# Branch A begun with two column tiles of half the tokens, and the entry of the FFN with its evictions, splits and sums in another order

## The chip, the core and the metric

The kernel runs on one core of a Trainium2 chip. The core has five engines that run side by side and meet through semaphores: TensorE (PE in the profile) multiplies matrices, VectorE (DVE) and ScalarE (ACT) work element by element, GpSimd (POOL) does a few element-wise operations and roots here, and SyncE (SP) only issues DMAs; ACT issues some too. PE writes its results to PSUM, which has eight banks of 128 partitions by 512 floats; everything else lies in SBUF. The metric is device time in microseconds (us) of one execution; lower is better.

## The reference, cut to what matters

One layer of a transformer-like block over 1024 tokens with 1024 channels, in float32. The two places that are changed lie behind the attention.

```python
y_a = stick_breaking_attention(q, k, v)
y_b = cb * causal_dwconv(cc * cx, conv_w[l])
merged = (jax.nn.sigmoid(ga) * (y_a @ w_branch_a[l])          # branch A
          + jax.nn.sigmoid(gb) * (y_b @ w_branch_b[l]))       # branch B
x = x + g1 * (merged @ w_out[l])                              # out-projection
h = rmsnorm(x, ln2_g[l]) * (1.0 + sc2) + sh2                  # FFN entry
f = (jax.nn.silu(h @ w_ffn_gate[l]) * (h @ w_ffn_up[l])) @ w_ffn_down[l]
return x + g2 * f
```

## The kernel before

**Products.** A float32 product is made of three matmuls: each operand is split into a high and a low part (`hi` is a rounded copy made by ACT, `lo` is the operand less `hi`, made by DVE), and `hi*hi`, `hi*lo` and `lo*hi` are summed in one PSUM bank. A matmul can therefore wait for an ACT copy or for the DVE subtraction behind it. In tile names `whi` and `wlo` are the parts of a weight; `rh`, `rl` and `big` hold those of activations.

**Branch A** (L1025 to L1042) computes, for each of eight column tiles `m` of the weight `w_a` and each half `n` of the tokens, one bank of 24 matmuls (eight blocks `k` of the inner dimension by three; `mm_ch`, L876 to L878). Two banks (`pj`) are there for it. DVE empties a bank with a multiplication by the gate (L1036: tile `sgi`, loaded by SP from DRAM, two buffers), adds branch B's part (L1037: tile `mb`, also a load) and ACT and DVE split the sum into `big` (L1041, L1042). A gate's buffer is free for the load after next once L1042 has read it. The operands `ya` come from the attention, whose last blocks for `n` = 1 are read back by SP (`yr`, L1017) and split (L1021 and its subtraction) while branch A is already running. A scheduler sets the order of instructions on each engine from the order of the source, with estimated costs and the buffers that are free; it already mixes the banks of (m, n) = (0, 1) and (1, 0).

**FFN entry** (from L1179). The out-projection goes over eight token tiles `i`. Each gives a new residual tile `x1`, an RMS norm (ACT squares and sums, L1209; POOL makes the root; ACT rescales, L1213), eight transposes on PE (`tail_tr`, L1094) into two banks, one for each half `g` of the channels, and eight evictions of 128x128 that scale and shift (`tail_ev`, ACT L1104 and DVE L1106) into the buffers `h2b`. `h2b` is a table of four: channel half by token half, names h2b00, h2b01, h2b10, h2b11. `tail_f` then does DVE subtractions between these and splits one (`rh[2]`, `rl[2]`, L1115).

The FFN's weights and activations are cut two by two, and each block product is formed with seven half-size products instead of eight, as in Strassen's scheme (Winograd's form). That takes sums of blocks: T3 = h2b11 - h2b00 (split into `rh[6]`, `rl[6]`, used by product 7) and T4 = h2b10 - h2b11 (split into `rh[3]`, `rl[3]`, used by product 4). A product is 12 matmuls (`half_prod`, L127 to L129). The first gate step's products are written by hand in the entry: `pq[1]`, `pq[2]`, then `pre[0, 1]`, `pre[1, 0]`, `pre[1, 1]` of three further weight tiles (their raw tiles `w_u[0]`, `w_g[1]`, `w_u[1]`, whose split halves are `s01`, `s10`, `s11`), then `pq[6]`, `pq[5]`, `pq[3]`, `pq[7]`; product 4 opens `strassen(0, 0)` behind it. `x1p`, `x11`, `x2p`, `x21` (tile name `wt`) collect partial results.

What stands between `i0` (at the last tile of the out-projection) and `in_order(i0)` (L1268) keeps, on each engine, the order in which it is written; the scheduler orders the rest around it. In the loop over gate steps behind it, ACT applies Silu to each gate tile (L1336), and POOL forms the sums of weight blocks (`ws`, L132) for gate steps from the second on.

Of the kernel before, what the change touches and what calls it, by code (L numbers as in the profile page):

```python
# [28 lines left out]
def block_kernel(tc, x, x_t, cols, ada_1, ada_2, ada_row, w_q, w_kv, w_v1, w_cg, w_a, w_b, w_o, w_g, w_u, w_d, out):  # L29
# [992 lines left out]
            tt(nc.vector, l_, yr, h_.bitcast(F32), ALU.subtract)  # L1022
            yah[n][k], yal[n][k] = h_, l_
    mh, mlo = [None] * 2, [None] * 2
    for m in range(KT):  # L1025
        if m == KT - 2:
            preload_wo()
        w = load_ch(w_a[m])
        for n in range(2):
            sa = fp.tile([P, 512], F32, tag="sgi", bufs=2, name=nm("sgi"))  # L1030
            nc.sync.dma_start(sa, d_sga[m, :, n * 512:(n + 1) * 512])
            mb = fp.tile([P, 512], F32, tag="st", bufs=3, name=nm("mb"))
            nc.sync.dma_start(mb, d_mb[m, :, n * 512:(n + 1) * 512])
            ps = ps_f()
            mm_ch(ps, w, yah[n], yal[n])
            nc.vector.tensor_tensor(out=sa, in0=ps, in1=sa, op=ALU.mult)  # L1036
            nc.vector.tensor_tensor(out=sa, in0=sa, in1=mb, op=ALU.add)  # L1037
            if m == 0:
                mh[n] = big()
                mlo[n] = big()  # L1040
            nc.scalar.activation(mh[n][:, m, :], sa, AF.Copy)  # L1041
            nc.vector.tensor_tensor(out=mlo[n][:, m, :], in0=sa, in1=mh[n][:, m, :].bitcast(F32), op=ALU.subtract)  # L1042
# [37 lines left out]
    def split_big(dh, dl, src, t=None):  # L1080

        if t is None:
            cuts = [(slice(k, k + 2), slice(0, 512)) for k in (0, 2)]
        else:
            cuts = [(slice(0, 4), slice(t * P, t * P + P))]
        for c in cuts:
            nc.scalar.activation(dh[:, *c], src[:, *c], AF.Copy)  # L1087
            tt(nc.vector, dl[:, *c], src[:, *c], dh[:, *c].bitcast(F32), ALU.subtract)
# [5 lines left out]
                nc.tensor.transpose(trs[g][:, j * P:(j + 1) * P], xn[:, (4 * g + j) * P:(4 * g + j + 1) * P], ident)  # L1094
        return trs

    def tail_ev(i, trs, acts=(0, 2)):
        n, t0 = i // 4, (i % 4) * P
        for g in range(2):
            for j in range(4):  # L1100
                k = 4 * g + j
                o, s = h2b[g][n][:, j, t0:t0 + P], trs[g][:, j * P:(j + 1) * P]
                if j in acts:
                    nc.scalar.activation(o, s, AF.Identity, scale=a2[:, k:k + 1], bias=mod[:, 2, k:k + 1])  # L1104
                else:
                    nc.vector.tensor_scalar(out=o, in0=s, scalar1=a2[:, k:k + 1], scalar2=mod[:, 2, k:k + 1],  # L1106
                                            op0=ALU.mult, op1=ALU.add)
# [44 lines left out]
    for ch in range(2):  # L1152
# [21 lines left out]
        for i in (0, 4, 1, 2, 3, 5, 6, 7) if ch else range(8):  # L1174
# [29 lines left out]
            nc.scalar.dma_start(x1[:, :512], d_x1[i, :, :512])  # L1204
            nc.vector.tensor_tensor(out=x1[:, cs], in0=tm, in1=xi, op=ALU.add)
# [3 lines left out]
            nc.scalar.activation(xn, x1, AF.Square, accum_out=ss)  # L1209
            r = rstd_of(ss, 1.0 / D, dp, 1)  # L1210
            if last:
                s01 = halves(load_raw(w_u[0]))
            nc.scalar.activation(xn, x1, AF.Copy, scale=r[:, 0:1])  # L1213
            tails.append((i, xn))
            if last:
# [17 lines left out]
    x1p, x11 = wt(1), wt(0)  # L1233
    nc.scalar.activation(x1p, pq[1], AF.Copy)
    tt(nc.vector, x11, pq[2], x1p, ALU.add)
    s10 = halves(load_raw(w_g[1]))
    trs7 = tail_tr(tails.pop()[1])
    s6.close()

# [15 lines left out]
    nc.scalar.activation(x2p, pre[0, 1][0], AF.Copy)
# [14 lines left out]
    s7 = ExitStack()  # L1270
    cp = s7.enter_context(tc.tile_pool(name="phc2", bufs=1, side="right", reuse_waits="tile"))
# [305 lines left out]
```

## Time and profile before

| what | value |
|---|---|
| median of 3 runs | 1859.14 us (1858.46 to 1859.62) |
| the profiled execution | 1862.36 us, of which the span of the instructions is 1860.6 us |
| PE busy | 1815.7 us, 98% of the span |
| DVE busy | 1351.7 us, 73% |
| ACT busy | 794.0 us, 43% |
| POOL busy | 369.3 us, 20% |

Times in the views count from the start of the span. A row of a timeline has the start, the duration, the engine, the line of the kernel, the operation, the tile written and the tiles read, the shape and how many alike were joined; in brackets stands how long the engine had been idle before, and what ended it. A duration of one matmul (0.39 us) overlaps the next: back-to-back matmuls of 128x512 start 0.2275 us apart. Likewise an operation of 128x512 on DVE or ACT is shown with 0.6 to 0.7 us and the next starts 0.52 (ACT) or 0.60 us (DVE) after it. Branch A runs from about 1017 to 1117 us, the out-projection to about 1210, the FFN entry to about 1262, the other gate and up products to about 1640, the down-projection to the end.

### The profile page before, as it was taken

The numbers are of one execution on the slowest core, as the hardware profiler recorded it, in microseconds if no ns is written. First come the engines' busy times: TensorE is split into PE (matmuls) and PEld (weight loads), VectorE is DVE, ScalarE is ACT, GpSimd is POOL, SyncE is SP. The second block draws the span as 40 slices with busy tenths as digits, with TensorE's granted clock in tenths as the row PEclk, the third lists the DMA queues.
The fourth block names the chain that finished last, engine by engine and source line by source line (L and its number), as shares of the span: only waits on it lengthen the run. The fifth ranks groups of instructions, "written<-read, shape, count | busy, mean of one in ns | idle before, by whom it ended". The sixth has DMA issues, their size and how long they took to land. (4 is left out here: it accounts for less than half of the span.)

```text
span 1860.6 us, 24885 instructions
## 1 busy us (share of the span) xinstructions
PE 1815.7 (98%) x8829; PEld 1505.1 (81%) x8829; DVE 1351.7 (73%) x1946; ACT 794.0 (43%) x1494; POOL 369.3 (20%) x277
## 2 busy tenths in 40 slices
PE   7999999999999999999999899989999999999999
PEld 4787778887879988888888788868888888878887
DVE  6873776779864888888887545589987787744776
ACT  4352553333343656665565211654444344422321
POOL 1043327423230000000000000104543444300000
PEclk9999999999999999999999999999999999999999
DMA  9598452227748565689544536414443334289766
GB/s 389 197 309 302 161 190 71 85 74 247 275 156 250 151 191 176 178 245 281 147 133 137 187 126 214 138 61 170 177 163 147 136 148 184 110 324 330 284 229 223
DMA packets 147267, 358.01 MB, mean 192 GB/s; under 512 B 15480, under 2 KB 44480, under 8 KB 144968
## 3 DMA queue, kind: packets, MB, share of 16 engines
q1 hardware_dynamic: 101816, 289.12, 46.1%
q10 hardware_dynamic: 44320, 63.64, 9.8%
q0 software_dynamic: 1008, 3.67, 0.5%
q8 instruction: 70, 1.15, 0.3%
q14 instruction: 53, 0.43, 0.1%
HBM read 245.74 MB, written 110.66 MB: 192 GB/s over the span
## 5 line engine op out<-in xcount | busy, mean ns | idle before, releaser
L788 DVE TENSOR_TENSOR_SCAN pt<-pt,mk 128x128 f32<-128x128 f32 (+7 forms) x128 | 172.0, 1350 | 48.2 <-ACT pt L784 48.0
L784 ACT ACTIVATE pt<-z,rq 128x512 f32<-128x512 f32 (+3 forms) x192 | 107.1, 579 | 88.6 <-PE z L783 57.5
L127 PE MATMUL e<-big,whi 128*128 128x512 f32 x352 | 137.7, 391 | 2.6 <-ACT whi L1070 2.5
L129 PE MATMUL e<-big,wlo 128*128 128x512 f32 x352 | 137.4, 390 | 0.9 <-DVE wlo L1071 0.8
L128 PE MATMUL e<-big,whi 128*128 128x512 f32 x352 | 137.2, 390 | 0.0
L118 POOL TENSOR_SCALAR rs_m<-ss 128x1 f32<-128x1 f32 x8 | 2.2, 280 | 661.1 <-ACT xn L1209 661.1
L132 DVE TENSOR_TENSOR c<-e,c 128x512 f32<-128x512 f32 x138 | 92.8, 686 | 53.6 <-PE e L129 51.7
L127 PE MATMUL pj<-big,whi 128*128 128x512 f32 x320 | 125.1, 391 | 1.0 <-DVE c L132 1.0
L128 PE MATMUL pj<-big,whi 128*128 128x512 f32 x320 | 124.7, 390 | 0.0
L129 PE MATMUL pj<-big,wlo 128*128 128x512 f32 x320 | 124.3, 390 | 0.0
L1404 PE MATMUL e<-whi,f 128*128 128x512 f32 (+1 forms) x319 | 121.8, 382 | 1.1 <-DMA f<-d_f 1.1
L1405 PE MATMUL e<-wlo,f 128*128 128x512 f32 (+1 forms) x319 | 121.8, 382 | 0.0
L1406 PE MATMUL e<-whi,f 128*128 128x512 f32 (+1 forms) x319 | 121.6, 382 | 0.0
L132 DVE TENSOR_TENSOR wlo<-raw,whi 128x512 fp32r<-128x512 f32 x116 | 89.1, 772 | 38.0 <-ACT whi L473 37.9
L132 DVE TENSOR_TENSOR c<-pj,c 128x512 f32<-128x512 f32 x140 | 93.2, 682 | 30.8 <-PE pj L129 30.6
L473 ACT ACTIVATE whi<-raw 128x512 fp32r<-128x512 f32 x116 | 72.7, 630 | 97.8 <-PE pj L128 42.8
L290 PE MATMUL pj<-whi,big 128*128 128x512 f32 x352 | 109.7, 398 | 4.2 <-ACT big L273 4.1
L132 POOL TENSOR_TENSOR ws<-raw,raw 128x512 f32<-128x512 f32 x40 | 55.3, 1384 | 287.7 <-DMA raw<-w_cg 126.4
L807 DVE TENSOR_TENSOR atl<-tr,ath 128x512 fp32r<-128x512 f32 (+1 forms) x192 | 99.6, 548 | 14.4 <-ACT ath L806 12.6
L127 PE MATMUL e<-rh,whi 128*128 128x512 f32 x264 | 104.1, 394 | 2.4 <-ACT rh L1087 2.4
L128 PE MATMUL e<-rl,whi 128*128 128x512 f32 x264 | 104.6, 396 | 1.3 <-DVE rl L132 1.3
L806 ACT ACTIVATE ath<-tr 128x512 fp32r<-128x512 f32 (+1 forms) x192 | 86.8, 489 | 44.0 <-PE o L818 25.8
(255 smaller groups left out, 5030.8 us busy)
## 6 DMA issues: line engine op xcount, KB each, us to landing
f<-d_f SPq DMA_DIRECT2D x77, 512.0 KB, 4.3
d_f<-fs SPq DMA_DIRECT2D x70, 512.0 KB, 3.3
raw<-w_cg SPq DMA_DIRECT2D x40, 512.0 KB, 5.1
raw<-w_u SPq DMA_DIRECT2D x26, 512.0 KB, 3.3
raw<-w_g SPq DMA_DIRECT2D x25, 512.0 KB, 3.5
ad<-ada ACTq DMA_DIRECT2D x19, 512.0 KB, 5.6
ada<-ada SPq DMA_DIRECT2D x8, 1024.0 KB, 10.3
d_t<-ts SPq DMA_DIRECT2D x16, 512.0 KB, 5.1
```

Of the source, the lines that this page charges most:

```text
L127: nc.tensor.matmul(ps, wh[:, k, :], fh[:, k, :], start=(k == 0), stop=False)
L128: nc.tensor.matmul(ps, wh[:, k, :], fl[:, k, :], start=False, stop=False)
L129: nc.tensor.matmul(ps, wl[:, k, :], fh[:, k, :], start=False, stop=(k == 3))
L132: eng.tensor_tensor(out=out, in0=a, in1=b, op=op)
L290: nc.tensor.matmul(ps, a, b, start=(k == 0 and q == 0), stop=(k == KT - 1 and q == 2))
L784: nc.scalar.activation(pt[:, off + s0:off + s0 + m], z[:, :m], AF.Sigmoid, scale=rq[:, 1, i, h:h + 1])
L788: nc.vector.tensor_tensor_scan(out=pt[:, rev], data0=pt[:, rev], data1=mk[:, rev], initial=1.0, op0=ALU.mult, op1=ALU.max)
L806: nc.scalar.activation(th[:, :nb, c0:c0 + P], src, AF.Copy)
L807: nc.vector.tensor_tensor(out=tl[:, :nb, c0:c0 + P], in0=src, in1=th[:, :nb, c0:c0 + P].bitcast(F32), op=ALU.subtract)
L1404: nc.tensor.matmul(o, sh, w[0][:, c], start=(j == 0), stop=False)
L1405: nc.tensor.matmul(o, sh, w[1][:, c], start=False, stop=False)
L1406: nc.tensor.matmul(o, sl, w[0][:, c], start=False, stop=(j == NJ - 1))
```

## The change

Three things in the source:

- Branch A takes its first four (m, n) in the order (0, 0), (1, 0), (0, 1), (1, 1) instead of (0, 0), (0, 1), (1, 0), (1, 1).
- `tail_ev` gives all four evictions of channel half `g` = 0 (one bank) to ACT and all four of `g` = 1 (the other bank) to DVE; before, both engines took two from each bank, in turns.
- In the FFN entry, the splits of `w_u[0]` come ahead of the last tile's Square, those of `w_g[1]` ahead of its rescaling, those of `w_u[1]` and of two weight sums (`sp3`, `sp4`) ahead of the last tile's evictions. T3 and T4 are subtracted in two halves of 128x1024 each, both ahead of the splits that read them, and the sum `x1p` comes ahead of T3's low part. The first Silu has to follow the end of the ordered region on ACT and DVE.

```diff
-    for m in range(KT):
-        if m == KT - 2:
+    wa = {}
+    for m, n in [(0, 0), (1, 0), (0, 1), (1, 1)] + [(m, n) for m in range(2, KT) for n in range(2)]:
+        if (m, n) == (KT - 2, 0):
             preload_wo()
-        w = load_ch(w_a[m])
-        for n in range(2):
-            sa = fp.tile([P, 512], F32, tag="sgi", bufs=2, name=nm("sgi"))
...
+        if n == 0:
+            wa[m] = load_ch(w_a[m])
+        sa = fp.tile([P, 512], F32, tag="sgi", bufs=2, name=nm("sgi"))
...
+        mm_ch(ps, wa[m], yah[n], yal[n])
...
-    def tail_ev(i, trs, acts=(0, 2)):
+    def tail_ev(i, trs):
+
         n, t0 = i // 4, (i % 4) * P
-        for g in range(2):
-            for j in range(4):
+        for j in range(4):
+            for g in range(2):
                 k = 4 * g + j
                 o, s = h2b[g][n][:, j, t0:t0 + P], trs[g][:, j * P:(j + 1) * P]
-                if j in acts:
+                if g == 0:
                     nc.scalar.activation(o, s, AF.Identity, scale=a2[:, k:k + 1], bias=mod[:, 2, k:k + 1])
...
+            if last:
+                s01 = halves(load_raw(w_u[0]))
...
             nc.scalar.activation(xn, x1, AF.Square, accum_out=ss)
             r = rstd_of(ss, 1.0 / D, dp, 1)
             if last:
-                s01 = halves(load_raw(w_u[0]))
+                s10 = halves(load_raw(w_g[1]))
             nc.scalar.activation(xn, x1, AF.Copy, scale=r[:, 0:1])
...
-    s10 = halves(load_raw(w_g[1]))
+    s11 = halves(load_raw(w_u[1]))
+    sp3, sp4 = split(ws0[3]), split(ws0[2])
     trs7 = tail_tr(tails.pop()[1])
...
     tail_ev(7, trs7)
     tail_f(7)
     pre[1, 0] = two(*s10)
-    s11 = halves(load_raw(w_u[1]))
     split_big(rh[5], rl[5], h2b[1][1])
-    sp3, sp4 = split(ws0[3]), split(ws0[2])
     pre[1, 1] = two(*s11)
...
-    tt(nc.vector, h2b[0][0], h2b[1][1], h2b[0][0], ALU.subtract)
+    for k in (slice(0, 2), slice(2, 4)):
+        tt(nc.vector, h2b[0][0][:, k], h2b[1][1][:, k], h2b[0][0][:, k], ALU.subtract)
+    tt(nc.vector, x1p, pq[6], x1p, ALU.add)
     split_big(rh[6], rl[6], h2b[0][0])
     pq[7] = product(sp4, 6)
     sp5 = split(load_raw(w_g[NJ])[:, 512:])
-    tt(nc.vector, x1p, pq[6], x1p, ALU.add)
-    tt(nc.vector, h2b[1][0], h2b[1][0], h2b[1][1], ALU.subtract)
+    for k in (slice(0, 2), slice(2, 4)):
+        tt(nc.vector, h2b[1][0][:, k], h2b[1][0][:, k], h2b[1][1][:, k], ALU.subtract)
     split_big(rh[3], rl[3], h2b[1][0])
-    in_order(i0)
+    ends = in_order(i0)
...
-            nc.scalar.activation(o, o, AF.Silu)
+            with tc.issue_after(ends[0]), tc.issue_after(ends[1]):
+                nc.scalar.activation(o, o, AF.Silu)
```

Where this moves instructions, the program's own rows show it. First DVE in branch A, around the evictions of the second and third bank. The bank and gate of (1, 0) are pj 10298 and sgi 10294 before, and 10263 and 10259 after; those of (0, 1) are 10253 and 10249 before, 10296 and 10292 after. Before:

```order
L132 TENSOR_TENSOR ya_2079_10201<-yr_2078_10199,ya_2079_10201 128x512
L1036 TENSOR_TENSOR sgi_2100_10294<-pj_2102_10298,sgi_2100_10294 128x512
L1036 TENSOR_TENSOR sgi_2090_10249<-pj_2092_10253,sgi_2090_10249 128x512
L1037 TENSOR_TENSOR sgi_2100_10294<-sgi_2100_10294,mb_2101_10296 128x512
L132 TENSOR_TENSOR wlo_2110_10367<-raw_2106_10360,whi_2109_10366 128x512
L1037 TENSOR_TENSOR sgi_2090_10249<-sgi_2090_10249,mb_2091_10251 128x512
```

and after (lines here are one higher):

```order
L132 TENSOR_TENSOR ya_2079_10201<-yr_2078_10199,ya_2079_10201 128x512
L1037 TENSOR_TENSOR sgi_2095_10259<-pj_2097_10263,sgi_2095_10259 128x512
L1038 TENSOR_TENSOR sgi_2095_10259<-sgi_2095_10259,mb_2096_10261 128x512
L1037 TENSOR_TENSOR sgi_2098_10292<-pj_2100_10296,sgi_2098_10292 128x512
L1043 TENSOR_TENSOR big_2089_10246<-sgi_2095_10259,big_2088_10245 128x512
L132 TENSOR_TENSOR wlo_2110_10367<-raw_2106_10360,whi_2109_10366 128x512
```

DVE empties (1, 0) first in both; (0, 1) is second in both. SP's rows keep their places, but the load that was for (0, 1)'s gate is now for (1, 0)'s, and the later one the other way round. Before, SP reads:

```order
L1031 DMA sgi_2090_10249<-d_sga_76 128x512
L1033 DMA mb_2091_10251<-d_mb_79 128x512
L1017 DMA yr_2078_10199<-d_ya1_75 128x512
L1033 DMA mb_2101_10296<-d_mb_79 128x512
L1033 DMA mb_2104_10329<-d_mb_79 128x512
L462 DMA raw_2117_10436<-w_a 128x1024
L1031 DMA sgi_2100_10294<-d_sga_76 128x512
```

and after:

```order
L1032 DMA sgi_2095_10259<-d_sga_76 128x512
L1034 DMA mb_2096_10261<-d_mb_79 128x512
L1017 DMA yr_2078_10199<-d_ya1_75 128x512
L1034 DMA mb_2099_10294<-d_mb_79 128x512
L1034 DMA mb_2104_10329<-d_mb_79 128x512
L462 DMA raw_2117_10436<-w_a 128x1024
L1032 DMA sgi_2098_10292<-d_sga_76 128x512
```

The gate that DVE asks for first is the one that SP loads first only after the change.

Second, ACT in the FFN entry, from tile 5's evictions (tiles h2b01 and h2b11) over the last tile's Square (writes xn and ss) to its rescaling (reads rs_r). Before:

```order
L1104 ACTIVATE h2b01_11198<-e_2323_11626,mod_113,a2_10860 128x128
L1104 ACTIVATE h2b11_11199<-e_2324_11627,mod_113,a2_10860 128x128 x2
L1115 ACTIVATE rh2_11193<-h2b11_11199 128x4x128
L1204 DMA x1_2330_11698<-d_x1_82 128x512
L1206 DMA d_x1_82<-x1_2330_11698 128x512
L1209 ACTIVATE xn_2332_11703,ss_2331_11702<-x1_2330_11698 128x1024
L1070 ACTIVATE whi_2336_11711<-raw_2335_11709 128x512
L1070 ACTIVATE whi_2338_11715<-raw_2335_11709 128x512
L1213 ACTIVATE xn_2332_11703<-x1_2330_11698,rs_r_2334_11706 128x1024
```

and after:

```order
L1106 ACTIVATE h2b01_11198<-e_2323_11626,mod_113,a2_10860 128x128 x4
L1217 ACTIVATE xn_2313_11582<-x1_2311_11577,rs_r_2315_11585 128x1024
L1117 ACTIVATE rh2_11193<-h2b11_11199 128x4x128
L1206 DMA x1_2330_11698<-d_x1_82 128x512
L1208 DMA d_x1_82<-x1_2330_11698 128x512
L1071 ACTIVATE whi_2332_11704<-raw_2331_11702 128x512
L1071 ACTIVATE whi_2334_11708<-raw_2331_11702 128x512
L1213 ACTIVATE xn_2337_11713,ss_2336_11712<-x1_2330_11698 128x1024
L1071 ACTIVATE whi_2341_11721<-raw_2340_11719 128x512
L1071 ACTIVATE whi_2343_11725<-raw_2340_11719 128x512
L1217 ACTIVATE xn_2337_11713<-x1_2330_11698,rs_r_2339_11716 128x1024
```

The high parts of `s01` (whi of `w_u[0]`) moved from behind the Square to ahead of it, and those of `s10` took their place.

Third, DVE at the end of the entry, from `rl[5]` (written to a big tile) on. Before, up to T4 (behind it come three low parts of weight sums and `rl[3]`):

```order
L132 TENSOR_TENSOR big_2356_11795<-h2b11_11199,big_2355_11794 128x1024 x2
L1071 TENSOR_TENSOR wlo_2365_11853<-wt_2196_10881,whi_2364_11852 128x512
L1071 TENSOR_TENSOR wlo_2367_11857<-wt_2195_10880,whi_2366_11856 128x512
L132 TENSOR_TENSOR wt_2371_11887<-e_2341_11745,wt_2370_11886 128x512
L132 TENSOR_TENSOR wt_2347_11767<-wt_2371_11887,wt_2347_11767 128x512
L132 TENSOR_TENSOR big_2356_11795<-h2b01_11198,big_2355_11794 128x1024 x2
L132 TENSOR_TENSOR h2b00_11200<-h2b11_11199,h2b00_11200 128x2048
L132 TENSOR_TENSOR rl6_11797<-h2b00_11200,rh6_11796 128x1024 x2
L1071 TENSOR_TENSOR wlo_2378_11954<-raw_2376_11951,whi_2377_11953 128x512
L132 TENSOR_TENSOR wt_2346_11766<-e_2372_11894,wt_2346_11766 128x512
L132 TENSOR_TENSOR h2b10_11201<-h2b10_11201,h2b11_11199 128x2048
```

and after, up to `rl[3]`:

```order
L132 TENSOR_TENSOR big_2365_11813<-h2b11_11199,big_2364_11812 128x1024 x2
L132 TENSOR_TENSOR wt_2371_11887<-e_2346_11755,wt_2370_11886 128x512
L132 TENSOR_TENSOR big_2365_11813<-h2b01_11198,big_2364_11812 128x1024 x2
L132 TENSOR_TENSOR h2b00_11200<-h2b11_11199,h2b00_11200 128x1024 x2
L132 TENSOR_TENSOR wt_2351_11776<-e_2372_11894,wt_2351_11776 128x512
L132 TENSOR_TENSOR rl6_11815<-h2b00_11200,rh6_11814 128x1024 x2
L1072 TENSOR_TENSOR wlo_2378_11956<-raw_2376_11953,whi_2377_11955 128x512
L132 TENSOR_TENSOR h2b10_11201<-h2b10_11201,h2b11_11199 128x1024 x2
L1072 TENSOR_TENSOR wlo_2391_12082<-ws_2198_10883,whi_2390_12081 128x512
L1072 TENSOR_TENSOR wlo_2394_12104<-ws_2197_10882,whi_2393_12103 128x512
L1072 TENSOR_TENSOR wlo_2397_12122<-ws_2199_10884,whi_2396_12121 128x512
L132 TENSOR_TENSOR rl3_11817<-h2b10_11201,rh3_11816 128x1024 x2
```

Two low parts (wlo) and one product of `wt` tiles have left this stretch: the low parts now come ahead of the last tile's evictions, the product behind `rl[3]`. The three low parts of weight sums ahead of `rl[3]` stand there in both.

More of the change, by code (lines that the diff above doesn't have):

```diff
@@ L1024, in block_kernel @@
     mh, mlo = [None] * 2, [None] * 2
-    for m in range(KT):
-        if m == KT - 2:
+    wa = {}
+    for m, n in [(0, 0), (1, 0), (0, 1), (1, 1)] + [(m, n) for m in range(2, KT) for n in range(2)]:
+        if (m, n) == (KT - 2, 0):
             preload_wo()
-        w = load_ch(w_a[m])
-        for n in range(2):
-            sa = fp.tile([P, 512], F32, tag="sgi", bufs=2, name=nm("sgi"))
[L1031 to L1042, printed above, removed]
+        if n == 0:
+            wa[m] = load_ch(w_a[m])
+        sa = fp.tile([P, 512], F32, tag="sgi", bufs=2, name=nm("sgi"))
+        nc.sync.dma_start(sa, d_sga[m, :, n * 512:(n + 1) * 512])
+        mb = fp.tile([P, 512], F32, tag="st", bufs=3, name=nm("mb"))
+        nc.sync.dma_start(mb, d_mb[m, :, n * 512:(n + 1) * 512])
+        ps = ps_f()
+        mm_ch(ps, wa[m], yah[n], yal[n])
+        nc.vector.tensor_tensor(out=sa, in0=ps, in1=sa, op=ALU.mult)
+        nc.vector.tensor_tensor(out=sa, in0=sa, in1=mb, op=ALU.add)
+        if m == 0:
+            mh[n] = big()
+            mlo[n] = big()
+        nc.scalar.activation(mh[n][:, m, :], sa, AF.Copy)
+        nc.vector.tensor_tensor(out=mlo[n][:, m, :], in0=sa, in1=mh[n][:, m, :].bitcast(F32), op=ALU.subtract)
     s3.close()
@@ L1082, in split_big @@
         if t is None:
-            cuts = [(slice(k, k + 2), slice(0, 512)) for k in (0, 2)]
+            cuts = [(slice(k, k + 2), slice(0, 512)) for k in range(0, src.shape[1], 2)]
         else:
```

## The prediction

> **What bounds the kernel now.** I read the page first: PE is busy for 98% of the span, so a gain can only come from its idle time or from its clock.
>
> ```profile
> span 1860.6 us, 24885 instructions
> PE 1815.7 (98%) x8829; PEld 1505.1 (81%) x8829; DVE 1351.7 (73%) x1946; ACT 794.0 (43%) x1494; POOL 369.3 (20%) x277
> ```
>
> Then busy time and granted clock in stretches of 3.41 us at both changed places (columns: stretch, its length, busy time of PE, its weight loads, DVE, ACT, POOL; PEclk; DMA share; GB/s).
>
> ```profile
> 1037.67:1041.09 3.42, 1.23 (x3) 0.48 (x3) 0.69 (x1) 0.87 (x2) 0.00 (x0) 1.00 0.71 240
> 1041.09:1044.50 3.41, 1.22 (x3) 1.03 (x4) 1.96 (x4) 0.04 (x1) 0.00 (x0) 0.50 0.02 9
> 1044.50:1047.91 3.41, 3.41 (x10) 2.67 (x9) 2.42 (x4) 1.22 (x2) 0.00 (x0) 0.50 0.69 219
> ...
> 1249.30:1252.71 3.41, 0.72 (x2) 0.19 (x1) 3.41 (x5) 1.95 (x3) 0.00 (x0) 1.00 0.35 135
> 1252.71:1256.12 3.41, 2.39 (x6) 1.91 (x7) 3.41 (x5) 0.60 (x3) 0.00 (x0) 0.50 0.00 0
> ...
> 1221.99:1225.40 3.41, 2.08 (x14) 1.60 (x12) 3.14 (x6) 2.36 (x5) 0.00 (x0) 1.00 0.00 0
> ```
>
> A long wait is paid twice: after the stretch with PE busy for 1.23 us (36%) the clock is half, and again after the one with 0.72 us (21%); after the one with 2.08 us (61%) it stays full. Half clock lasts until a full stretch has passed.
>
> **Branch A, the wait.** PE's timeline:
>
> ```profile
> 1037.97 0.50 PE L876 MATMUL pj<-ya,whi 128*128 128x512 f32 x1 [1.07 <-ACT ya L1021]
> ...
> 1043.29 0.80 PE L876 MATMUL pj<-ya,whi 128*128 128x512 f32 x1 [3.86 <-DVE sgi L1036]
> ...
> 1048.05 0.40 PE L878 MATMUL pj<-ya,wlo 128*128 128x512 f32 x1
> ```
>
> The eviction that ends the 3.86 us waits itself for a gate (DVE's and SP's timelines, and the loads' times in the view of the tile `sgi`):
>
> ```profile
> 1037.94 0.69 DVE L132 TENSOR_TENSOR ya<-yr,ya 128x512 fp32r<-128x512 f32 x1 [1.83 <-ACT ya L1021]
> 1042.54 1.29 DVE L1036 TENSOR_TENSOR sgi<-pj,sgi 128x512 f32<-128x512 f32 x2 [3.90 <-DMA sgi<-d_sga]
> ```
>
> ```profile
> 1030.66 0.50 SPq L1031 DMA_DIRECT2D sgi<-d_sga  x1
> ...
> 1035.18 0.43 SPq L1031 DMA_DIRECT2D sgi<-d_sga  x1
> ```
>
> ```profile
> DMA to landing us min/median/max: 2.9/3.8/7.2
> ```
>
> The gate issued at 1035.18 is (1, 0)'s. It lands near 1042.5, the longest of its kind, and DVE wants it first. (0, 1)'s gate, issued at 1030.66, has lay there since about 1035 (median 3.8, at most 1037.9), but its eviction stands behind. So both banks stay full.
>
> **What the new order does.** SP's rows stay; the gate of 1030.66 becomes (1, 0)'s, which DVE evicts first. (1, 0) also runs ahead on PE, and its bank is full before (0, 1)'s last block, which still needs the `ya` of 1037.94. DVE therefore evicts (1, 0) right behind that row, at 1037.94 + 0.60 = 1038.54 to 1039.23. PE ends (0, 1) at about 1039.3 as now and goes on with (1, 1) at 1039.3 instead of 1043.29: **4.0 us**. Next is the late gate, now (0, 1)'s: landing still at 1042.5, eviction done at 1043.25. PE wants that bank for (2, 0) after 24 x 0.2275 = 5.46 us, at 1044.75, which leaves 1.5 us. The low part of (1, 0) now stands on DVE behind that late eviction, so the buffer for (1, 1)'s gate is free at 1043.9; issued at 1044 it lands at 1047.8 (median) or 1051.2 (longest), and (2, 1) wants the bank at 1050.2. By the median there is nothing to pay, by the longest 1.7 us. I take nothing.
>
> The second price: 11 starts from 1043.29 to 1048.05 take 4.76 us instead of 11 x 0.2275 = 2.50, so half clock costs 2.26. With no wait above 1.07 us the stretch is busy enough: **2.2 us** back. A start of (0, 1) on a bank that comes free 0.2 us later is deducted: branch A gives 6.0 us; between 2.3 (half clock stays and the late landing is paid: 4.0 - 1.7) and 6.5.
>
> **FFN entry, the waits.** PE's timeline again, then ACT's:
>
> ```profile
> 1217.18 0.50 PE L127 MATMUL e<-big,whi 128*128 128x512 f32 x1 [0.92 <-ACT whi L1070]
> ...
> 1225.64 0.50 PE L127 MATMUL e<-big,whi 128*128 128x512 f32 x1 [1.57 <-ACT whi L1070]
> ...
> 1233.25 0.50 PE L129 MATMUL e<-big,wlo 128*128 128x512 f32 x1 [0.80 <-DVE wlo L1071]
> ...
> 1249.13 0.39 PE L129 MATMUL e<-rh,wlo 128*128 128x512 f32 x1
> 1251.87 0.51 PE L127 MATMUL e<-rh,whi 128*128 128x512 f32 x1 [2.35 <-ACT rh L1087]
> 1253.73 0.80 PE L128 MATMUL e<-rl,whi 128*128 128x512 f32 x1 [1.35 <-DVE rl L132]
> 1254.32 0.63 PE L129 MATMUL e<-rh,wlo 128*128 128x512 f32 x1
> ...
> 1259.44 0.44 PE L129 MATMUL e<-big,wlo 128*128 128x512 f32 x1
> ```
>
> ```profile
> 1209.43 0.79 ACT L1104 ACTIVATE h2b<-e,mod,a 128x128 f32<-128x128 f32 x2
> 1210.70 0.46 ACT L1104 ACTIVATE h2b<-e,mod,a 128x128 f32<-128x128 f32 x1 [0.48 <-DVE h2b L1106]
> ...
> 1215.46 1.06 ACT L1209 ACTIVATE xn<-x 128x1024 f32<-128x1024 f32 x1 [3.19 <-DVE x L1205]
> ...
> 1216.52 1.14 ACT L1070 ACTIVATE whi<-raw 128x512 fp32r<-128x512 f32 x2
> ```
>
> Start to start less 0.2275, with the slower starts behind a stall, the three stalls up to 1233.25 and their small followers cost about 4.6 us. The first is `s01`, behind the Square; the second `s10`, behind the whole of tile 6; the third `s11`, behind tile 7.
>
> The evictions first. In turns on one bank, ACT waits for DVE (0.48) and DVE for ACT, about 0.53 each time. On two banks at once they are 4 x 0.32 = 1.3 us per tile; that both engines read two banks at full speed is not in these rows, so the other bound is the alternation as now. I take 1.3. The Trainium skill ("PSUM — Partial Sum Buffer", specifications) says that ScalarE and VectorE read PSUM in parallel at full bandwidth as long as they don't meet in a bank; by it the first bound would hold and the second fall away. No row here shows that pairing.
>
> With it tile 7's residual is ready about 1.9 us before the 1215.46 at which the Square could start. `s01`'s two highs (1.04) go first, at 1213.6 to 1214.6, and its lows end by 1215.3; PE wants them at 1216.1. The Square starts 1.9 - 1.04 = 0.9 us earlier than now; `s10` covers POOL's root, and `s10` and `s11` are split 5 us or more before their products. All three stalls go, and PE would be at product 4 at 1249.13 + 0.23 - 4.6 = 1244.8.
>
> **FFN entry, the chain on DVE.** DVE's timeline:
>
> ```profile
> 1226.98 0.41 DVE L1106 TENSOR_SCALAR h2b<-e,a,mod 128x128 f32<-128x128 f32 x1
> 1228.78 0.76 DVE L1106 TENSOR_SCALAR h2b<-e,a,mod 128x128 f32<-128x128 f32 x2 [1.39 <-ACT h2b L1104]
> 1230.07 0.41 DVE L1106 TENSOR_SCALAR h2b<-e,a,mod 128x128 f32<-128x128 f32 x1 [0.53 <-ACT h2b L1104]
> ...
> 1233.72 2.36 DVE L132 TENSOR_TENSOR big<-h2b,big 128x1024 fp32r<-128x1024 f32 x2
> 1236.00 1.29 DVE L1071 TENSOR_TENSOR wlo<-wt,whi 128x512 fp32r<-128x512 f32 x2
> 1237.95 0.69 DVE L132 TENSOR_TENSOR wt<-e,wt 128x512 f32<-128x512 f32 x1 [0.67 <-ACT wt L1255]
> ...
> 1244.97 2.36 DVE L132 TENSOR_TENSOR rl<-h2b,rh 128x1024 fp32r<-128x1024 f32 x2 [1.13 <-ACT rh L1087]
> ...
> 1248.45 2.28 DVE L132 TENSOR_TENSOR h2b<-h2b,h2b 128x2048 f32<-128x2048 f32 x1
> ...
> 1252.45 2.36 DVE L132 TENSOR_TENSOR rl<-h2b,rh 128x1024 fp32r<-128x1024 f32 x2
> ```
>
> From tile 7's first eviction to `rl[3]` DVE needs 1252.45 - 1226.98 = 25.5 us. Out of it go the waits for ACT, 1.39 + 0.53 + 0.67 + 1.13 = 3.7 (the last since T3's first half reaches ACT 1.1 us sooner, with `x1p` as cover), the two low parts of `sp3` and `sp4`, 1.2, and the product of `wt` tiles, 0.6: 20.0 remain. The halves cost nothing: two of 128x1024 are 2 x 1.14 (row 1244.97 is such a pair), one of 128x2048 is 2.28. `s11`'s lows leave it too, but then DVE waits as long for ACT's first half of `rh[5]`, which they covered. Tile 7 itself starts earlier by 1.9 (tile 6) + 1.1 (its two alternations) less 1.2 (the low parts now ahead): 1.8, at 1225.2. `rl[3]` starts at 1245.2, and PE's second matmul of product 4, 1.28 us behind as in 1252.45 to 1253.73, at about 1246.2 (the slack of 0.1 us between dependent operations goes with the removed ones). That is 7.6 us before 1253.73; PE, there at 1245.0, still waits some 1.2 us. Bounds: 4.3, where evictions still alternate for three tiles (3 x 1.1 later), and 8.7, where PE finds `rl[3]` ready.
>
> That wait leaves PE busy for at least 2.1 of 3.41 us, like the stretch after which the clock stayed full. Half clock then goes: 12 starts from 1254.32 to 1259.44 take 5.12 us instead of 2.73, **2.4 us**. FFN entry: 7.6 + 2.4 = **10.0 us**.
>
> POOL's sums for the second gate step come next:
>
> ```profile
> 1260.04 1.29 POOL L132 TENSOR_TENSOR ws<-raw,raw 128x512 f32<-128x512 f32 x1 [42.52 <-DMA raw<-w_g]
> ```
>
> Their weight needs a buffer that DVE frees behind `rl[3]`, 7.3 us earlier than now, while PE comes 10.0 earlier: 2.7 us of cover are lost. There are 5.6 now: four sums of 1.3 and a split of 1.2 end at 1266.4, and PE comes to them after product 4 (to 1258.4) and five products of 12 x 0.2275, at 1272.0. The Silu held back with its table load (ACT, about 1.9 us in the middle of the entry) lands where ACT idles. Both at nothing.
>
> **Sum.** 6.0 + 10.0 = 16.0 us. The profiled execution took 1862.36, 1.8 around the span included; it would be 1846.4. The median of the runs is 3.2 lower, 1859.14, and the forecast **1843.1 us**.
>
> **Rivals.**
> - *The clock drops at the wait that is left* (chance 0.15). A wait of 1.2 to 2 us leaves PE busy between 41% and 65% of a stretch, and between 36% and 61% no row tells. Price 2.4, once: 1845.5; in both places 1847.7. The Trainium skill ("TensorE: Matmul & The Clock Gate", Part 1) wants about one idle window of 3.4 us before half clock. By it neither 1037.67 nor 1249.30, in which PE still worked, should have been followed by half clock; they were, so the rows decide.
> - *The late gate is the new wait in branch A* (0.08): it comes 1.5 us later still or (1, 1)'s takes 7.2. PE waits 1.7 and more, half clock with it: branch A gives 2 instead of 6, 1847.
> - *DVE stays the bound of the entry* (0.10): evictions alternate or ACT is late with `rh[3]`; 4.3 instead of 7.6, and half clock stays: 1843.1 + 3.3 + 2.4 = 1848.8.
> - *The change doesn't do what it says* (0.03): the scheduler had already mixed (0, 1) and (1, 0), and T3 and T4 cost DVE as much as before. Then both waits stay: 1859. Against it: the gate that DVE asks for first does change.
> - *Slower, through the clock* (0.04): many short waits in the first gate steps, as POOL's sums come late, hold PE at half clock. Half clock costs 3.41 / 2 = 1.7 us a stretch; from ten stretches in a row (34 us) it eats the 16.0, from twelve it loses 4: 1863. Against it: before, it lasted two stretches each time. The Trainium skill ("TensorE: Matmul & The Clock Gate", A second HAM failure mode) tells of a clock that swings when PE idles briefly between groups; no row here shows it.
>
> **Chances.** The forecast has 0.60, the rivals 0.15, 0.08, 0.10, 0.03 and 0.04. About 0.2% (3.7 us) is what a measurement of this kernel can tell from no change. The first four cases are faster: 0.93; 0.03 the same, 0.04 slower. The range reaches down to 1839.5 (product 4 without a wait, 1.1; branch A's 6.5; and 2 for the difference between a profiled execution and the runs) and up to 1850.5, which holds all faster cases with the same 2 us above the worst.
>
> **What would show it.** After: PE without the wait of 3.86 at L1037's release, (1, 1) starting 4 us sooner, clock 1.00 there; no stall at `s01`, `s10`, `s11`; one wait of about 1.2 us on `rl[3]`. Wrong it would be if a wait on a gate or on POOL's `ws` stood in their place, or half clock at either.

## The result, and the profile after

| kernel | median (runs) | ratio to before, 95% interval |
|---|---|---|
| before | 1859.4 us (4); 1860.9 us (15, in the last comparison) | |
| changed, first comparison | 1848.4 us (4: 1846.7 to 1852.2) | 0.9938 [0.9924, 0.9952] |
| changed, timed again | 1850.3 us (6: 1847.7 to 1852.5) | 0.9945 [0.9932, 0.9957] |

The change makes the kernel some 10.7 us faster; 16.0 were forecast, and 1843.1 us. The time lies within the range, in its upper half; the second timing's median, 1850.3 us, is just below the range's end of 1850.5. The profiled execution took 1846.74 us, the fastest of the changed kernel's ten. The page of after:

```profile
span 1845.0 us, 24888 instructions
PE 1810.0 (98%) x8829; PEld 1504.7 (82%) x8829; DVE 1346.3 (73%) x1948; ACT 792.1 (43%) x1494; POOL 369.1 (20%) x277
```

PE issues the same 8829 matmuls in both kernels, so both timelines of PE can be laid side by side by the number of the matmul. What the changed kernel gains on before's profiled execution between two numbers is what it gains in that place:

| place (numbers of the matmuls) | gain | forecast |
|---|---|---|
| 0 to 5200, programs alike up to branch A | 4.8 us | 0 |
| branch A (5200 to 5400) | 6.3 | 6.0 |
| out-projection (5400 to 6000) | 0.0 | 0 |
| FFN entry up to product 4 (6000 to 6200) | 10.4 | 10.0 |
| next gate steps (6200 to 6400) | -3.8 | 0 |
| start of the down-projection (7800 to 8000) | -2.1 | 0 |

Both places gave what was forecast of them. What was missing stands behind the entry, and in how typical one execution is. PE's timeline of after, all waits at branch A and from the entry on to the third gate step:

```profile
1025.07 0.50 PE L876 MATMUL pj<-ya,whi 128*128 128x512 f32 x1 [0.36 <-DVE mb L948]
1032.96 0.49 PE L876 MATMUL pj<-ya,whi 128*128 128x512 f32 x1 [0.57 <-ACT ya L1021]
1033.69 0.50 PE L877 MATMUL pj<-ya,whi 128*128 128x512 f32 x1 [0.23 <-DVE ya L132]
...
1234.93 0.50 PE L128 MATMUL e<-rl,whi 128*128 128x512 f32 x1 [1.37 <-DVE rl L132]
...
1266.77 0.50 PE L127 MATMUL e<-big,whi 128*128 128x512 f32 x1 [1.63 <-DVE c L132]
...
1271.77 0.50 PE L127 MATMUL e<-big,whi 128*128 128x512 f32 x1 [1.99 <-ACT c L1310]
```

The wait of 3.86 us in branch A is gone, and so are the stalls on the three split weights; on `rl[3]` 1.37 us are left (forecast 1.2). The last two rows are new: each is the first matmul into a PSUM bank that an eviction has just freed. Before, PE came to the second of these banks as it was being freed, and waited some 0.3 us (before's timelines of ACT and of PE):

```profile
1288.85 0.58 ACT L1305 ACTIVATE c<-e 128x512 f32<-128x512 f32 x1
```

```profile
1289.49 0.50 PE L127 MATMUL e<-big,whi 128*128 128x512 f32 x1
```

DVE's timeline of after, first in branch A:

```profile
1032.94 0.69 DVE L132 TENSOR_TENSOR ya<-yr,ya 128x512 fp32r<-128x512 f32 x1 [0.88 <-ACT ya L1021]
1033.55 0.68 DVE L1037 TENSOR_TENSOR sgi<-pj,sgi 128x512 f32<-128x512 f32 x1
...
1037.48 0.69 DVE L1037 TENSOR_TENSOR sgi<-pj,sgi 128x512 f32<-128x512 f32 x1 [2.52 <-DMA sgi<-d_sga]
```

(1, 0) is evicted right behind the last `ya`, as worked out; the late gate, now (0, 1)'s, keeps DVE for 2.52 us, and PE waits for nothing there. Then the queue of DVE and of ACT ahead of the two new waits:

```profile
1260.95 3.48 DVE L132 TENSOR_TENSOR fs<-wt,fs 128x512 fp32r<-128x512 f32 x2
1264.35 1.76 DVE L1072 TENSOR_TENSOR wlo<-ws,whi 128x512 fp32r<-128x512 f32 x1
1266.04 0.68 DVE L132 TENSOR_TENSOR c<-e,c 128x512 f32<-128x512 f32 x1
...
1270.41 0.68 DVE L132 TENSOR_TENSOR fs<-c,fs 128x512 fp32r<-128x512 f32 x1
```

```profile
1271.12 0.60 ACT L1310 ACTIVATE c<-e 128x512 f32<-128x512 f32 x1 [0.17 <-DVE fs L132]
```

The eviction at 1266.04 (`c<-e`) stands behind 5 us of splits of hidden activations (`fs`) and of a weight, which nobody waits for so soon. ACT's copy at 1271.12 wants to write the tile `c1` (tag c10, one buffer), which DVE's split at 1270.41 still reads. The banks are those of `pre[1, 0]` and `pre[1, 1]`, products that the entry makes ahead for the second gate step: they hold four of the eight banks until the first gate step's hidden activations are through (which banks and tiles these are follows from the source and from what ended the waits; the experiment with a second c1 tests it).

### The profile page after: what moved, and what is told of

Its sections match the earlier page's. It is cut to its first block, busy times and chain, and to the rows that moved or that the text cites. A ratio compares the mean times of both kernels' runs of the same rounds, so it can differ in the third digit from the quotient of the medians.

```text
span 1845.0 us, 24888 instructions
## 1 busy us (share of the span) xinstructions
PE 1810.0 (98%) x8829; PEld 1504.7 (82%) x8829; DVE 1346.3 (73%) x1948; ACT 792.1 (43%) x1494; POOL 369.1 (20%) x277
## 4 chain that ended last, share of the span: by engine, by line
PE 80%; DVE 11%; DMA 5%; issue 2%; ACT 2%; POOL 1%; SPq 0%; ACTq 0%; DVEq 0%; POOLq 0%
PE e L129 7%; PE e L128 7%; PE e L127 7%; PE pj L290 5%; PE pj L127 5%; PE pj L129 5%; PE pj L128 5%; PE pj L876 4%; PE pj L877 4%; PE pj L878 4%; PE e L1411 4%; PE e L1412 4%; PE e L1410 4%; PE tr L803 3%; PE o L819 2%
## 5 line engine op out<-in xcount | busy, mean ns | idle before, releaser
L127 PE MATMUL pj<-big,whi 128*128 128x512 f32 x320 | 125.1, 391 | 0.4 <-DVE c L132 0.4
L128 PE MATMUL pj<-big,whi 128*128 128x512 f32 x320 | 124.7, 390 | 0.0
L876 PE MATMUL pj<-big,whi 128*128 128x512 f32 x256 | 103.9, 406 | 0.0
## 6 DMA issues: line engine op xcount, KB each, us to landing
ada<-ada SPq DMA_DIRECT2D x8, 1024.0 KB, 10.4
```

Source lines behind the costliest of these rows:

```text
L127: nc.tensor.matmul(ps, wh[:, k, :], fh[:, k, :], start=(k == 0), stop=False)
L128: nc.tensor.matmul(ps, wh[:, k, :], fl[:, k, :], start=False, stop=False)
L876: nc.tensor.matmul(ps, wh, rh_, start=(k == 0), stop=False)
```

## The experiments

For all runs: gain on before's profiled execution by place, from PE's matmuls as above, and the medians.

| run | median us (runs) | ratio, 95% interval | branch A | entry | gate steps behind |
|---|---|---|---|---|---|
| a1_again: changed | 1850.3 (6) | 0.9945 [0.9932, 0.9957] | 5.7 | 10.4 | -3.8 |
| e1: branch A alone | 1855.4 (5) | 0.9968 [0.9956, 0.9981] | 5.2 | 1.3 | -3.4 |
| e2: entry alone | 1852.1 (5) | 0.9953 [0.9941, 0.9965] | 1.4 | 10.4 | -2.7 |
| e5: changed, second c1 | 1846.2 (5) | 0.9922 [0.9910, 0.9934] | 5.0 | 10.4 | 0.5 |
| u1: changed, old evictions | 1856.6 (10) | 0.9978 [0.9968, 0.9987] | 6.4 | 5.0 | -7.2 |
| u2: changed, old sums | 1852.1 (4) | 0.9950 [0.9934, 0.9966] | 5.6 | 7.7 | -1.2 |
| u3: changed, old splits | 1852.7 (4) | 0.9956 [0.9941, 0.9971] | 5.7 | 10.3 | -5.4 |
| e3: changed, Silu free | 1851.5 (4) | 0.9951 [0.9937, 0.9964] | 6.7 | 7.4 | -1.9 |
| e7: e5, lows held | 1846.1 (4) | 0.9922 [0.9908, 0.9937] | 6.9 | 10.4 | 0.2 |
| e8: e5, old splits | 1843.0 (4) | 0.9906 [0.9891, 0.9921] | 7.0 | 10.3 | 0.5 |
| e9: e5, old sums | 1843.9 (4) | 0.9910 [0.9896, 0.9925] | 6.4 | 7.7 | 0.5 |
| e10: before, second c1 | 1858.7 (11) | 0.9990 [0.9980, 1.0001] | 2.5 | 0.1 | 0.5 |

### The same again, and each half of the change alone

The changed kernel, nothing edited:

> The changed kernel once more, timed longer. Theory: branch A gives 6.3 us and the entry up to product 4 gives 10.3, of which two waits in the next gate steps (1.6 us, ended by DVE, and 2.0 us, ended by ACT) hand 3.6 back, so that 13 are left against a before without half clock at 522 us: 1846 to 1849. Both waits stand in its profile again, whatever the clock does elsewhere. Rival (the two waits are an accident of one execution): they are missing here, and the median falls to 1843 to 1845.

Measured 1850.3 us. Both waits stand there again to the hundredth, 1.63 and 1.99 us, so they are the program's and not one execution's; the rival falls. The median lies above the 1846 to 1849 expected.

Branch A alone in the kernel before:

```diff
-    for m in range(KT):
...
-        for n in range(2):
...
+    for m, n in [(0, 0), (1, 0), (0, 1), (1, 1)] + [(m, n) for m in range(2, KT) for n in range(2)]:
```

> The kernel before with branch A's new order alone. Theory: the late gate and the half clock behind it are there in every execution of before, so 6 us come back and nothing is handed on: 1853, with PE's wait of 3.9 us on the eviction gone. Rival (the late landing of 7.2 us was bad luck of the profiled execution): 2 us or less, 1857 to 1859.

Measured 1855.4 us, 5.6 less than before and above the 1853 expected. The wait is gone and the place gives 5.2 us, but something is handed on, against the expectation. PE's timeline of this run:

```profile
1282.64 0.50 PE L127 MATMUL e<-big,whi 128*128 128x512 f32 x1 [1.96 <-ACT c L1306]
```

In this execution half clock in the entry lasted one stretch instead of two (a gain of 1.3 us there), so PE came to the held bank earlier and met it still full: 1.96 us, and half clock behind it. So before, too, was near this limit; its stalls in the entry covered it.

The entry's edits alone (the kernel after with branch A's old loop):

```diff
-    for m, n in [(0, 0), (1, 0), (0, 1), (1, 1)] + [(m, n) for m in range(2, KT) for n in range(2)]:
+    for m in range(KT):
...
+        for n in range(2):
...
```

> The kernel before with the FFN entry's edits alone. Theory: 10.3 us up to product 4, 3.6 handed back in the two waits behind it: 6.7, about 1852.5. Rival (nothing is handed back when branch A is not changed too, since PE arrives later): 10, about 1849.

Measured 1852.1 us: 10.4 in the entry and 2.7 handed back (the theory had 3.6), in the same two waits, 1.17 and 1.42 us. Branch A, whose program here is that of before, is 1.4 us better than in before's profiled execution:

```profile
1040.88 0.50 PE L876 MATMUL pj<-ya,whi 128*128 128x512 f32 x1 [2.76 <-DVE sgi L1036]
```

2.76 us of wait instead of 3.86, and one stretch of half clock instead of two (e10 has 2.21 and one stretch). The late gate is not equally late each time.

### What holds the banks

A second buffer for the tile c1:

```diff
-        c21, c12, c22 = (ct(f"c{q}{e}", 1) for q in range(1, 4))
+        c21, c12, c22 = (ct(f"c{q}{e}", 2 if q == 1 else 1) for q in range(1, 4))
```

> The changed kernel with a second buffer for the tile c1 of each gate step (the first sum of a step, tags c10 and c11). Theory: the two waits come from PSUM banks of the products made ahead (pre[1, 0] and pre[1, 1]), whose evictions wait for this tile and for DVE's queue; with a second tile both waits go and 3.6 us come back: 1844 to 1845. Rival (DVE as a whole is the limit in the first gate step, 32 of 35 us busy): the waits only move to another bank and 0 to 1 us comes back: 1847 to 1848.

Measured 1846.2 us, 4.1 below the changed kernel in the same comparison, but above the 1844 to 1845 expected. Both waits are gone, and the place gives 0.5 instead of -3.8. Timelines of PE, of DVE and of ACT in this run; the first row is PE's only wait between 1200 and 1310 us:

```profile
1240.83 0.50 PE L128 MATMUL e<-rl,whi 128*128 128x512 f32 x1 [1.36 <-DVE rl L132]
```

```profile
1258.74 1.78 DVE L132 TENSOR_TENSOR fs<-c,fs 128x512 fp32r<-128x512 f32 x1
1260.44 1.78 DVE L132 TENSOR_TENSOR wt<-c,c 128x512 f32<-128x512 f32 x1
```

```profile
1243.09 0.58 ACT L1310 ACTIVATE c<-e 128x512 f32<-128x512 f32 x1
...
1246.68 0.58 ACT L1310 ACTIVATE c<-e 128x512 f32<-128x512 f32 x1
```

ACT's copies of these products now come at 1243.1 and 1246.7, where the changed kernel had them at 1260.2 and 1271.1, and DVE's adding of `pre[1, 1]` follows ahead of most of the hidden activations. DVE is no less busy (33.1 of the 35 us from 1236 us on, against 32.5 of the 35 from 1240 us on in after), and its operations beside POOL still take 1.78 instead of 0.68 us: its load was not the limit, the order and the single buffer were.

The control, the same line in the kernel before:

> The kernel before with the second c1 tile alone. Theory (before, PE's own stalls in the entry cover the held banks; the one wait there is 0.29 to 0.53 us): 0 to 0.5 us, 1860.4 to 1861. Rival (the tile helps by itself, whatever the entry does): 3 to 4 us, 1857.

Measured 0.9990 [0.9980, 1.0001]: 0.5 us in the place, as expected. The tile is worth 4 us only once PE comes early. (The median is 2.2 us lower, branch A's late gate included.)

### The parts of the entry, undone one by one

The evictions as before, both engines on each bank:

```diff
-        for j in range(4):
-            for g in range(2):
+        for g in range(2):
+            for j in range(4):
...
-                if g == 0:
+                if j in acts:
```

> The changed kernel with the evictions as before (both engines in turns on each bank), all else new. Theory of the prediction: 1.1 us a tile for tiles 5, 6 and 7 come back onto DVE's chain, so rl[3] is 3.3 us later, PE waits 4.6 instead of 1.37 there, half clock (2.4) follows, and the entry's 10.4 us fall to about 4.7; total 1852 to 1854. Rival (ACT and DVE read their banks no faster side by side than in turns): rl[3] at the same time, 10.4 stays.

The entry falls to 5.0 us (4.7 expected), and 7.2 are handed back, more than in any other run. So the time, 1856.6 us, lies above the 1852 to 1854 expected. PE's timeline:

```profile
1228.34 0.49 PE L127 MATMUL e<-big,whi 128*128 128x512 f32 x1 [1.19 <-ACT big L1088]
1229.60 0.50 PE L128 MATMUL e<-big,whi 128*128 128x512 f32 x1 [0.77 <-DVE big L132]
...
1244.56 0.50 PE L128 MATMUL e<-rl,whi 128*128 128x512 f32 x1 [2.06 <-DVE rl L132]
...
1282.04 0.80 PE L127 MATMUL e<-big,whi 128*128 128x512 f32 x1 [4.53 <-ACT c L1309]
```

The lateness shows already at product 6 (`rh[5]` and `rl[5]`, in big tiles), and part of what was expected at `rl[3]` is taken there. Counted from the end of the out-projection, `rl[3]` starts 5.3 us later than in after, not 3.3. PE has no wait on `s01`, `s10` or `s11` here, though the evictions are the old ones. With 1856.6 us the other edits together are worth only 4 us without this one, branch A's included.

The sums T3 and T4 whole, `x1p` behind them:

```diff
-    for k in (slice(0, 2), slice(2, 4)):
-        tt(nc.vector, h2b[0][0][:, k], h2b[1][1][:, k], h2b[0][0][:, k], ALU.subtract)
-    tt(nc.vector, x1p, pq[6], x1p, ALU.add)
+    tt(nc.vector, h2b[0][0], h2b[1][1], h2b[0][0], ALU.subtract)
...
-    for k in (slice(0, 2), slice(2, 4)):
-        tt(nc.vector, h2b[1][0][:, k], h2b[1][0][:, k], h2b[1][1][:, k], ALU.subtract)
+    tt(nc.vector, x1p, pq[6], x1p, ALU.add)
+    tt(nc.vector, h2b[1][0], h2b[1][0], h2b[1][1], ALU.subtract)
```

> The changed kernel with T3 and T4 subtracted whole and x1p where it was. Theory: DVE waits 1.1 us for ACT's first half of rh[6] again, rl[3] is about 1 us later, PE waits 2.4 instead of 1.37; without half clock the entry gives 9.4, with it 7. Rival (the halves cost DVE as much as they save): 10.4 stays.

PE's timeline of this run:

```profile
1240.58 0.49 PE L127 MATMUL e<-rh,whi 128*128 128x512 f32 x1 [0.83 <-ACT rh L1088]
1242.42 0.50 PE L128 MATMUL e<-rl,whi 128*128 128x512 f32 x1 [1.35 <-DVE rl L132]
```

2.2 us of wait instead of 1.37, half clock behind it, and 7.7 for the entry. But only 1.2 are handed back: 6.5 together, as much as the changed kernel keeps (10.4 - 3.8 = 6.6). By these places, the banks take back all that this edit gains.

The splits at their old places, behind Square, tile 6 and tile 7:

```diff
-            if last:
-                s01 = halves(load_raw(w_u[0]))
...
-                s10 = halves(load_raw(w_g[1]))
+                s01 = halves(load_raw(w_u[0]))
...
-    s11 = halves(load_raw(w_u[1]))
-    sp3, sp4 = split(ws0[3]), split(ws0[2])
+    s10 = halves(load_raw(w_g[1]))
...
+    s11 = halves(load_raw(w_u[1]))
     split_big(rh[5], rl[5], h2b[1][1])
+    sp3, sp4 = split(ws0[3]), split(ws0[2])
```

> The changed kernel with the splits of s01, s10, s11, sp3 and sp4 at their old places. Theory: the three stalls come back (0.9, 1.6 and 0.8 and what follows them, 4.6 together at most), less the 1.37 that PE then needn't wait at rl[3], and rl[3] moves by the 1.2 us of the two low parts: the entry gives 7 to 8.5. Rival (two-bank evictions alone take the stalls away): 10.4 stays.

The theory falls: the entry gives 10.3, and PE's only wait in it is this one:

```profile
1242.35 0.50 PE L128 MATMUL e<-rl,whi 128*128 128x512 f32 x1 [1.44 <-DVE rl L132]
```

No stall on `s01`, `s10` or `s11`. With the evictions on two banks the splits are early enough in either order. The run with the old evictions shows the other half: there the new order alone takes the three stalls away too. By matmul 6100, behind the place of the last stall, PE has gained 5.0 us in the entry in after and in this run, and 4.6 in that one. What this run loses (-5.4) are the waits on the banks, 1.64 and 1.99 us, with half clock behind the second.

The first Silu without the rule that holds it:

```diff
-            with tc.issue_after(ends[0]), tc.issue_after(ends[1]):
-                nc.scalar.activation(o, o, AF.Silu)
+            nc.scalar.activation(o, o, AF.Silu)
```

> The changed kernel without the rule that holds the first Silu behind the entry. Theory (the hold is worth nothing by itself): ACT's table load and Silu, 1.9 us, come in ahead of rh[5]'s source and the product of wt tiles, 0.6, comes back into DVE's chain: rl[3] 0.6 to 1.5 us later, PE's wait there 2 to 2.9, the entry gives 9 to 10, and the waits behind shrink by as much: 1850 to 1851, as the changed kernel. Rival (the held Silu, late on ACT, makes the two bank waits): they go and 3.6 come back: 1847.

1851.5 us, not to be told from the changed kernel. In the entry it costs more than expected: PE waits 2.49 us on `rl[3]`, half clock follows, and 7.4 are left; behind it 1.9 are handed back instead of 3.8. The rival falls: both bank waits are still there, shorter (0.85 and 0.92).

### With the banks free

The old splits, with the second c1 tile:

> The second c1 tile, with the splits at their old places. Theory (the new places of the splits are worth nothing, since the evictions on two banks alone had taken the three stalls away): 10.3 at product 4 and no wait behind it, 1846 to 1847 as with the new places. Rival (the new places pay further on): a wait of 1 us or more in the next gate steps, 1848 or more.

1843.0 us, with 10.3 and 0.5 in the two places: the new places of the splits are worth nothing here. By place it is the equal of e5. Its median is 3 us lower; between the two profiled executions the difference lies before the entry (branch A 7.0 against 5.0, and no half clock near 520 us), where the orders are alike. For the medians that is not shown.

The whole sums, with the second tile:

> The second c1 tile, with T3 and T4 subtracted whole and x1p where it was. Theory (what the entry gains is kept once no bank is held behind it): the 1 us on rl[3] and the half clock behind it, 2.7 together, are now paid in full: 1848.5 to 1849. Rival (DVE's whole load sets the time, whatever PE's waits in the entry): as with the second tile alone, 1846 to 1847.

By place as expected, 7.7 and 0.5: the 2.7 us are now lost in full. The median doesn't show it: 1843.9 us (1841.4 to 1846.7). Differences of 3 us between these variants are no larger than what executions of one program differ by elsewhere, so the medians don't settle which of e5, e7, e8 and e9 is best. The medians of all four lie below both of the changed kernel's, though only the interval of e8 lies clear of both of its intervals; e8, with the lowest median, is 17.9 us below before.

Last, e5 with the three low parts ahead of `rl[3]` held behind it. The edit holds the subtractions of the splits of `strassen(0, 1)`:

```diff
-        los.append(nc.vector.tensor_tensor(out=lo, in0=src, in1=hi.bitcast(F32), op=ALU.subtract))
+        with ExitStack() as st_:
+            for i_ in held:
+                st_.enter_context(tc.issue_after(i_))
+            los.append(nc.vector.tensor_tensor(out=lo, in0=src, in1=hi.bitcast(F32), op=ALU.subtract))
...
+        held[:] = [e_ for e_ in ends if e_.engine == nc.vector.engine] if j == 0 else []
```

> The changed kernel with the second c1 tile, and with the low parts of up weight sums in the first step (three of them stood on DVE ahead of rl[3]) held behind rl[3]. Theory (those three, 1.8 us, are what is left of PE's wait on rl[3]): the wait of 1.36 us goes, the second c1 tile keeps the gain, 1843 to 1845 where the second c1 tile alone has 1846. Rival (ACT's rh[3] is next in line, or the gain is handed back in the first gate step again): 1846 to 1847.

1846.1 us: the rival. PE's timeline, its only wait from 1230 to 1260 us:

```profile
1243.78 0.50 PE L127 MATMUL e<-big,whi 128*128 128x512 f32 x1 [1.35 <-DVE c L132]
```

The wait on `rl[3]` is gone and one of the same length has come at the next product, on a bank that DVE empties behind those three. DVE's work up to there is the same in either order.

## Why the prediction was right, and where not

- **Branch A, "4.0 us" and "2.2 us" back.** Right against the profiled execution: 5.0 to 7.0 us in the runs with the new order, on average 6.1. Against before's other executions it is less. Its program ran in three traces, with losses of 0, 1.4 and 2.5 us less than in the one that the sum was made from; on average 1.3. So the change is worth about 4.8 there. The step that failed is in the sum: "The median of the runs is 3.2 lower". That offset came from three runs; over 15 it is 1.5, and the profiled execution's wait and half clock were among the larger ones.
- **Evictions at 1.3 us a tile on two banks at once.** Right. Four of ACT and four of DVE lie side by side in after (timelines of ACT and DVE):

```profile
1206.19 1.49 ACT L1106 ACTIVATE h2b<-e,mod,a 128x128 f32<-128x128 f32 x4
```

```profile
1205.95 1.36 DVE L1108 TENSOR_SCALAR h2b<-e,a,mod 128x128 f32<-128x128 f32 x4
```

  The Trainium skill ("PSUM — Partial Sum Buffer", specifications) has both engines at full bandwidth on different banks; the trace agrees.
- **"All three stalls go".** They went, but the prediction counted on evictions and splits together, and either alone is enough: PE has none of the three stalls with the old order of the splits (u3) and none with the old evictions (u1). Beside the new evictions the new order of the splits is worth nothing (u3, e8).
- **`rl[3]` 7.6 us sooner, product 4 waiting 1.2, half clock gone.** Measured 7.7, 1.37 and no half clock, and for the entry 10.4 us for 10.0. The halves of T3 and T4, with `x1p` as cover, are worth 2.7 by place (u2, e9).
- **"Both at nothing"**, for what comes behind the entry. Here the sum failed, by 3.8 us. The prediction asked whether POOL's sums would be in time (they were: no wait on `ws`) and where the held Silu would fall (it makes no wait, e3). It did not ask which banks PE would find. Up to product 4 PE had gained 10.4 us, but DVE less: `rl[3]` starts at 1233.66 instead of 1252.45, 18.8 us earlier, of which 11.1 had been gained before the entry, so 7.7. DVE's row of after:

```profile
1233.66 2.36 DVE L132 TENSOR_TENSOR rl<-h2b,rh 128x1024 fp32r<-128x1024 f32 x2
```

  The other 2.7 of PE's are half clock that is gone, which DVE's rows never felt (2.36 us for `rl[3]` in both kernels). In the first gate step DVE evicts, splits and sums almost without a pause (31.9 of 36 us before, 32.5 of 35 after), and from the start of `rl[3]` to ACT's copy that lets PE have the second bank 37.5 us pass instead of 36.4 (1271.12 and 1288.85 are the copies; the product of `wt` tiles, 0.6, now stands in there). In both kernels PE waits for that copy, so it keeps only what the copy gained, which is 2.7 + 1.1 = 3.8 us less than the 10.4. A second buffer gives it back (e5).
- **The rest.** 4.8 + 10.4 - 3.8 = 11.4, against 10.7 measured. The down-projection's first wait on `f` from DRAM (1.08 us before) was 1.84 in after's profile with half clock behind it, and 0.97 in the next: it differs from run to run, and nothing ties it to the change.
- **Rivals.** The clock did not drop at the wait that was left. None of the five had the mechanism that cost 3.8 us; "DVE stays the bound" had the engine, but looked for it in the entry; the last one had the place, the first gate steps, but looked at POOL.
- **Slips in its working.** They change nothing above: 1253.73 less 1246.2 is 7.5, not 7.6, and 2 us above the worst faster case (1848.8) is 1850.8, not 1850.5. Branch A's upper bound of 6.5 has no sum behind it, and three runs lie above it (6.7 to 7.0).

## What to carry to other kernels

When a stall goes, follow each buffer that the engine behind it will want next (PSUM banks above all), and ask by how much the engine that frees it gains: PE keeps only that much. An edit that pays at its own place can be worth nothing in the end, as the halved sums were, until one more buffer lets the gain through. And where a wait hangs on a DMA, or brings half clock, look at more than one execution before pricing it.

## What the runs showed of the hardware

**The clock.** The prediction left open what happens between 36% and 61% of a stretch. The fourteen traces (before's, after's and those of the twelve runs) now show it. In each of them all changes of the clock from 100 us on lie a whole number of stretches of 3.41 us apart, so the trace can be cut into these stretches. Every one with PE busy for less than 44% is followed by half clock (30 of them). Behind a stretch at full clock with PE busy for 51% or more the clock stays full, but for one (59%, near 830 us of e3); between, both occur. Once the clock is half, more is needed to end it than the prediction's rows could tell: stretches with PE busy for 70% (before, from 1252.7 us) and 78% (u1, from 1281.3) were followed by another at half, one with 86% (u1, from 520.1) by full clock. Two views of stretches, of after and of u2:

```profile
1264.48:1267.89 3.41, 1.78 (x8) 1.14 (x8) 3.41 (x3) 0.00 (x0) 2.36 (x2) 1.00 0.49 197
1267.89:1271.31 3.42, 1.89 (x9) 1.23 (x7) 3.42 (x7) 2.38 (x5) 0.00 (x0) 1.00 0.29 104
1626.35:1629.76 3.41, 1.57 (x8) 1.02 (x7) 3.41 (x7) 0.63 (x1) 0.54 (x1) 1.00 0.54 185
1629.76:1633.18 3.42, 3.42 (x10) 2.64 (x9) 3.32 (x7) 1.16 (x2) 1.05 (x2) 0.50 0.88 273
```

```profile
1239.90:1243.31 3.41, 1.38 (x5) 0.94 (x6) 3.41 (x5) 3.38 (x4) 0.00 (x0) 0.99 0.00 0
1243.31:1246.73 3.42, 3.42 (x10) 2.66 (x9) 3.42 (x7) 2.04 (x5) 0.00 (x0) 0.51 0.11 20
```

Busy for 1.78 and 1.89 us (52% and 55%), the clock stays full; for 1.57 and 1.38 (46% and 40%) it is halved in the next stretch. A wait of 1.6 to 2 us can therefore go either way by where it falls in the stretch: the one of 1.99 us left the clock full in after and in a1, and halved it in u3. The Trainium skill ("TensorE: Matmul & The Clock Gate", Part 1) asks for about one idle window; the runs show that a little over half of one is enough.

**DVE beside POOL.** While POOL sums two SBUF tiles, DVE's operations on two SBUF tiles take 1.7 to 1.8 us instead of 0.68, and those that read PSUM 0.68 as ever. DVE's timeline and POOL's, of after:

```profile
1250.53 1.77 DVE L132 TENSOR_TENSOR c<-c,c 128x512 f32<-128x512 f32 x1
1252.23 0.68 DVE L132 TENSOR_TENSOR c<-e,c 128x512 f32<-128x512 f32 x1
```

```profile
1250.00 1.76 POOL L132 TENSOR_TENSOR ws<-raw,raw 128x512 f32<-128x512 f32 x1 [3.54 <-DVE c L132]
1251.72 1.75 POOL L132 TENSOR_TENSOR ws<-raw 128x512 f32<-128x512 f32 x1
```

The Trainium skill ("GPSIMD Engine Reference", Specifications) has the SBUF interfaces of the two shared for such operations; the slowdown agrees. What it costs this kernel was not tried.
